# Column tiles of the input projection computed by pairs in seven block products, with weight sums made by accumulating loads

## The chip, the cores and the metric

The kernel runs on one core of a Trainium2 chip. The metric is the device time of one execution in microseconds, the median of several runs. The engines are TensorE (PE, matmul), VectorE (DVE), ScalarE (ACT), GpSimd (Pool) and SyncE (SP); SP and Pool also issue DMAs, Pool through a queue whose descriptors it writes itself, and all DMAs share the core's 16 DMA engines.

## The reference

One layer of a hybrid decoder over 528 prompt tokens (16 of them meta tokens) and 32 sample tokens (8 sequences of 4):

```python
h = rmsnorm(x, g_pre)                                       # 560 x 2048
q, k, v, ga, cb, cc, ch, gc, ma, mc = split(h @ w_in)        # 2048 x 12288
a = stick_breaking(q, k, v) * silu(ga)                       # 8 heads of 128; the samples read 4 cached pages each
c = cb * causal_conv3(cc * ch) * silu(gc)                    # 1024 channels
m = sigmoid(ma + b_ga) * (a @ w_pa) + sigmoid(mc + b_gc) * (c @ w_pc)
x = x + rmsnorm(m @ w_out, g_post)
```

The sections q, k, v, ga, cb, cc, ch, gc are 1024 columns wide, ma and mc 2048. Everything is in float32. The keys, the values and the last rows of the conv's input are outputs too.

## The kernel before

Activations lie transposed in SBUF: `h_hi` and `h_lo` are [128, 16, 560], model width on the partitions in 16 contraction tiles, tokens along the free dimension. Each float32 value is kept as hi + lo, two numbers in TensorE's fp32r format, and a product is three matmuls: whi·h_hi, whi·h_lo, wlo·h_hi.

`proj(c, ranges)` makes one column tile of 128 columns of `h @ w_in`. `weights` (L180) loads the tile's weights as two blocks of 1024 x 128 (512 KB each, issued by SP into one of three `raw` buffers), casts hi on ACT (L188) and subtracts lo on DVE (L189), into one of four hi and lo buffers. `gemm_into` (L192) then runs 16 contraction tiles x 3 matmuls for each of two token ranges, 96 matmuls of 128 x 272 or so (L201), into two PSUM blocks. 256 such 1024 x 128 blocks of weights are split this way.

In the order of the program: the norm; the eight `ga` tiles; eight heads (k, v, q tiles, then the prompt's attention, whose chain of log, sums over keys, exponent and product with the values is L396 to L460); the tile pair cc, ch of conv channel tile 0 (`conv_in(0)`); a loop over 16 pairs of gate tiles `ma`, `mc`, which stores the gates in DRAM (`gate_scr`) and after each column tile takes one step of the generator `decode_steps`; the other conv tiles (`conv_in(1)` to `conv_in(7)`), then `gc` and `cb` for each of 8 channel tiles. Decode reads the pages of the cache: for each of 8 sequences the queries are broadcast to all partitions (`qb`), each of four pages (`page`, 128 keys x 1024) is multiplied with four queries on DVE, and reduced by head on DVE (L560) or ACT (L556); after that come the softmax-like chain and the products with the value pages.

The conv result `c_raw` stays in SBUF and is split to `c_hl` in place; attention's result is loaded from DRAM (`a_scr`, through `arl`) and split to `a_hl` (L305, L306) beside the last `gc`, `cb` tiles. Then come the tiles of `a @ w_pa` and `c @ w_pc`, two and two in turn, 48 matmuls each, merged with the gates to `m1` and `m2`; the product with `w_out`; norm and residual.

A scheduler places each engine's instructions by priority in the order of the program, as far as buffers and waits allow; pools of the program (`heads`, `gates`, `dec`) hold SBUF, and what a later pool allocates in the same place waits until the earlier is free.

Of the kernel before, what the change touches and what calls it, by code (L numbers as in the profile page):

```python
# [25 lines left out]
MID = 288                # tokens [.., MID) and [MID, T) go to two PSUM banks  # L26
ALL = ((0, MID), (MID, T))
QRY = ((NMETA, MID), (MID, T))           # tokens whose outputs are asked for
CNV = ((NMETA - 2, MID), (MID, T))       # these and the conv history before them
TQ = T - NMETA           # 544  # L30
PQ = SEQ                 # prompt tokens among them
# [5 lines left out]
EPS = 1e-6  # L37
LNEXP = "natural_log_exp_and_others"
# [6 lines left out]
def hybrid_step_kernel(  # L45
# [21 lines left out]
    wraw = ctx.enter_context(tc.tile_pool(name="wraw", bufs=3))  # L67
    whl = ctx.enter_context(tc.tile_pool(name="whl", bufs=4))
# [15 lines left out]
    # -------------------------------------------------------------- constants  # L84
# [17 lines left out]
    def load_x(xt, i):  # L102
        lo, hi = XT[i]
        if i == 0:
            nc.sync.dma_start(xt[0:NMETA, :], meta_tokens)
            nc.sync.dma_start(xt[NMETA:hi, :], xp[0:hi - NMETA, :])
        elif hi <= TP:
            nc.sync.dma_start(xt, xp[lo - NMETA:hi - NMETA, :])
        else:
            nc.sync.dma_start(xt[0:TP - lo, :], xp[lo - NMETA:SEQ, :])  # L110
            nc.sync.dma_start(xt[TP - lo:hi - lo, :], xs)
# [21 lines left out]
    # g_pre on every partition, by a product with ones  # L133
# [70 lines left out]
    def gemm(units, rhs, ranges):  # L204
        """rhs(k) -> (hi, lo) of contraction tile k, by token. Returns a PSUM block per token range."""
# [13 lines left out]
    def parts(outs, ranges, base=0):  # L219
        """(PSUM block, slice of a tile whose column 0 is token `base`) of each range."""  # L220
        return [(o, slice(t0 - base, t1 - base)) for o, (t0, t1) in zip(outs, ranges)]

    # the first two gates start on the first tokens while the others are normalized
    START = ((NMETA, 2 * P), (2 * P, T))
# [21 lines left out]
    # small tables: per-channel columns by a transpose of row-wise loads  # L246
# [25 lines left out]
    # -------------------------------------------------- scratch kept in DRAM  # L272
    sg_scr = dram.tile([H, P, PQ], F32, name="sg_scr")
    a_scr = dram.tile([H, P, PQ], F32, name="a_scr")
    gate_scr = dram.tile([KD, P, 2, TQ], F32, name="gate_scr")
    q_scr = dram.tile([TS, DA], F32, name="q_scr")

    # persistent sample-side pieces
# [3 lines left out]
    v_new = const.tile([TS, H, P], F32, name="v_new")  # L282
# [12 lines left out]
    # ---------------------------------------------------------------- heads  # L295
    ictx = ExitStack()
    yp_ = ictx.enter_context(tc.tile_pool(name="cin", bufs=1))
    gctx = ExitStack()
    gp = gctx.enter_context(tc.tile_pool(name="gates", bufs=2))
# [12 lines left out]
    def natural(raw, nat, nat_s):  # L312
        """raw [128, T] -> nat [128, 5, 128] (prompt rows), nat_s [32, 128] (sample rows)."""
# [10 lines left out]
    # key tile -> (group, column in the group, width, first query token, keys)  # L324
# [10 lines left out]
    def head(h):  # L335
        # k
# [4 lines left out]
        for ob, s in parts(o, ALL):  # L341
            act.copy(kr[:, s], ob)
            split_evac(khi[:, s], klo[:, s], kr[:, s], kr[:, s])
# [7 lines left out]
        # v  # L351
        o = proj(GATE_V + h * P, ALL)
        vr = hp.tile([P, T], F32, name="raw", bufs=1)
        for ob, s in parts(o, ALL):
            act.copy(vr[:, s], ob)
        vn = hp.tile([P, 5, P], F32, name="nat", bufs=1)
        natural(vr, vn, v_new[:, h, :])
# [6 lines left out]
        pool.dma_start(v_sample[0, :, :, h, :].rearrange("b t d -> (b t) d"), v_new[:, h, :])  # L364
        # q, scaled
# [3 lines left out]
        for ob, s in parts(o, QRY):  # L369
            split_evac(qhi[:, s], qlo[:, s], ob, ob, SCALE)  # L370
        qs = hp.tile([P, TS], F32, name="qs", bufs=1)
        act.activation(qs, o[1][:, TP - MID:T - MID], AF.Copy, scale=SCALE)
# [5 lines left out]
        # logits of the new keys for the sample queries  # L378
# [7 lines left out]
        # prompt attention: key tiles by later queries, grouped by PSUM bank  # L386
# [24 lines left out]
        for g in GROUPS:  # L411
# [9 lines left out]
            if g == "C":  # L421
                # sums of the later key tiles, key by key
# [44 lines left out]
    for h in range(H):  # L467
        o = ga_o[h] if h < 2 else proj(GATE_GA + h * P, QRY)
        sg = hp.tile([P, TQ], F32, name="sg", bufs=2)
        for ob, s in parts(o, START if h < 2 else QRY, NMETA):  # L470
# [7 lines left out]
    UP, US = PQ + 2, DB * (DT + 2)  # L478
    C0 = NMETA - 2

    def conv_in(i, y):
        cp = yp_
        """u = cc * ch of channel tile i, its last rows out, y = conv(u) + bias."""
        o = proj(COL_CC + i * P, CNV)
        cc = cp.tile([P, T - C0], F32, name="cc", bufs=1)
        for ob, s in parts(o, CNV, C0):
            act.copy(cc[:, s], ob)
        o = proj(COL_CH + i * P, CNV)
        u = cp.tile([P, UP + US], F32, name="u", bufs=1)
        up = u[:, 0:UP]  # L490
        us = u[:, UP:].rearrange("p (b t) -> p b t", t=DT + 2)
        act.copy(us[:, :, 0:2], stc[:, i, :].rearrange("p (b r) -> p b r", r=2))
        dve.tensor_mul(up[:, 0:MID - C0], o[0], cc[:, 0:MID - C0])
        dve.tensor_mul(up[:, MID - C0:UP], o[1][:, 0:TP - MID], cc[:, MID - C0:UP])
        dve.tensor_mul(us[:, :, 2:], o[1][:, TP - MID:T - MID].rearrange("p (b t) -> p b t", t=DT),
                       cc[:, UP:].rearrange("p (b t) -> p b t", t=DT))
        for yv, uv, sl in ((y[:, 0:PQ], up, lambda q: (slice(None), slice(q, q + PQ))),
# [373 lines left out]
```

## Time and profile before

| | |
|---|---|
| median of 3 runs | 1734.3 us (1733.22 to 1734.79) |
| the profiled execution | span 1736.9 us, 2.6 us above that median (no other time is listed for it) |
| PE busy | 1706.4 us, 98% |
| DVE, ACT, Pool busy | 842.8, 744.7, 202.2 us |
| DMA | 249.87 MB, 144 GB/s over the span |

The time by stages, in us of the span, with PE's busy time in each:

| stage | from, to | PE busy |
|---|---|---|
| norm and first tiles | 0 to 66 | 47.8 |
| heads | 66 to 543 | 477 |
| gates with decode's logits | 543 to 944 | 401 |
| conv_in 1 to 7, rest of decode | 944 to 1147 | 203 |
| gc, cb, then w_pa and w_pc | 1147 to 1536 | 389 |
| w_out, norm, residual | 1536 to 1737 | 188.6 |

A busy share is an average over stages. PE has almost no idle time outside the first and the last stage, so the time of a stage in between is read as a number of matmuls. The granted clock of TensorE was 0.996 over the span. Rows that name a line L give that line of the kernel before.

### The profile page before, as it was taken

To read this page: it belongs to the slowest core of one execution; us is meant where nothing else is said; L and a number is where in the kernel's file an instruction comes from. 1 tells how busy PE (TensorE), PEld (TensorE's weight loads), DVE (VectorE), ACT (ScalarE), POOL (GpSimd) and SP (SyncE) were. 2 spreads that over 40 slices of the span, in tenths; PEclk is the share of its full clock that TensorE was granted. 3 is DMA by queue.
4 is the path that set the end of the run, shared out by engine and by line. 5 is a ranking of instruction groups with operands and counts; after the bars stand their busy time and mean duration, and the time that the engine had idled before them with its cause. 6 is when DMAs were issued, how large, how long until landed. Compare 5 with 4: busy or idle time off the path is not lost.

```text
span 1736.9 us, 32151 instructions
## 1 busy us (share of the span) xinstructions
PE 1706.4 (98%) x12764; PEld 1637.0 (94%) x12764; DVE 842.8 (49%) x2092; ACT 744.7 (43%) x2026; POOL 202.2 (12%) x345
## 2 busy tenths in 40 slices
PE   5999999999999999999999999999999999999997
PEld 4999999999999999999999878899999999999986
DVE  7322554554445999996123222242224554444464
ACT  4322555455454999886223111132223222244543
POOL 5000222122111111111001111010000000000010
PEclk9999999999999999999999999999999999999999
DMA  6333333333325777774343444343233444567584
GB/s 191 94 110 116 88 99 93 87 88 98 99 82 192 247 257 253 248 244 148 111 120 102 166 160 149 121 139 91 80 98 85 137 127 133 164 166 184 174 260 153
DMA packets 302057, 249.87 MB, mean 144 GB/s; under 512 B 9181, under 2 KB 272145, under 8 KB 298721
## 3 DMA queue, kind: packets, MB, share of 16 engines
q1 hardware_dynamic: 278992, 161.89, 32.0%
q0 software_dynamic: 22912, 85.91, 14.2%
q8 instruction: 100, 1.64, 0.4%
q14 instruction: 51, 0.42, 0.1%
q10 hardware_dynamic: 2, 0.01, 0.0%
HBM read 225.42 MB, written 22.36 MB: 143 GB/s over the span
## 4 chain that ended last, share of the span: by engine, by line
PE 95%; DVE 2%; DMA 2%; ACT 0%; issue 0%; SPq 0%; POOLq 0%; POOL 0%; ACTq 0%; DVEq 0%
PE mm L201 83%; PE z L631 2%; PE z L830 2%; PE mm L830 2%; PE z L450 1%; DMA raw<-in_w_out 1%; PE o L460 1%; PE z L396 1%; PE o L830 1%; DMA raw<-in_w_in 1%; DVE hn L164 0%; PE tp L830 0%; PE tp L316 0%; DVE h_lo L177 0%; PE z L785 0%; DVE rtmp L120 0%
## 5 line engine op out<-in xcount | busy, mean ns | idle before, releaser
L201 PE MATMUL mm<-h_hi,wlo 128*128 128x272 f32 (+4 forms) x3072 | 894.1, 291 | 0.0
L201 PE MATMUL mm<-h_hi,whi 128*128 128x272 f32 (+4 forms) x3072 | 892.9, 291 | 0.0
L201 PE MATMUL mm<-h_lo,whi 128*128 128x272 f32 (+4 forms) x3072 | 888.1, 289 | 0.3 <-DVE h_lo L177 0.2
L201 PEld LDWEIGHTS mm<-h_hi,whi 128*128 128x128 f32 x3072 | 580.7, 189 | 9.3 <-issue 6.7
L201 PEld LDWEIGHTS mm<-h_hi,wlo 128*128 128x128 f32 x3072 | 580.0, 189 | 4.1 <-issue 3.4
L201 PEld LDWEIGHTS mm<-h_lo,whi 128*128 128x128 f32 x3072 | 579.2, 189 | 4.8 <-issue 3.4
L189 DVE TENSOR_TENSOR wlo<-raw,whi 128x1024 fp32r<-128x1024 f32 x252 | 308.4, 1224 | 493.7 <-ACT whi L188 492.3
L188 ACT CAST whi<-raw 128x1024 fp32r<-128x1024 f32 x256 | 269.0, 1051 | 518.0 <-PE mm L201 499.8
L556 ACT ACTIVATE junk<-pr 128x128 f32<-128x128 f32 x512 | 150.7, 298 | 7.1 <-DVE pr L553 4.3
L560 DVE CUSTOM_DVE_ANT_0 prod<-page,qb 128x128 f32<-128x128 f32 x512 | 116.2, 285 | 1.0 <-DMA qb<-q_scr 1.0
L201 PE MATMUL mm<-m,whi 128*128 128x288 f32 x512 | 105.8, 301 | 0.0
L556 ACT ACTIVATION_READ_ACCUMULATOR junk<-pr 128x1 f32 x512 | 97.2, 190 | 0.0
L201 PE MATMUL mm<-c_hl,whi 128*128 128x272 f32 x512 | 96.8, 287 | 0.0
L201 PE MATMUL mm<-a_hl,whi 128*128 128x272 f32 x512 | 96.7, 288 | 0.0
L201 PEld LDWEIGHTS mm<-m,whi 128*128 128x128 f32 x512 | 84.0, 193 | 0.0
L553 DVE TENSOR_TENSOR pr<-page,qb 128x1024 f32<-128x1024 f32 x64 | 78.0, 1220 | 6.2 <-ACT junk L556 5.7
L201 PEld LDWEIGHTS mm<-c_hl,whi 128*128 128x128 f32 x512 | 80.7, 188 | 0.0
L201 PEld LDWEIGHTS mm<-a_hl,whi 128*128 128x128 f32 x512 | 80.5, 189 | 0.0
L201 PE MATMUL mm<-m,wlo 128*128 128x288 f32 x256 | 76.6, 299 | 0.0
L201 PE MATMUL mm<-c_hl,wlo 128*128 128x272 f32 x256 | 74.2, 290 | 0.0
L201 PE MATMUL mm<-a_hl,wlo 128*128 128x272 f32 x256 | 73.9, 289 | 0.0
L804 DVE TENSOR_TENSOR wlo<-raw,whi 128x1024 fp32r<-128x1024 f32 x32 | 39.1, 1224 | 38.4 <-ACT whi L803 37.9
(289 smaller groups left out, 1641.6 us busy)
## 6 DMA issues: line engine op xcount, KB each, us to landing
raw<-in_w_in SPq DMA_DIRECT2D x192, 512.0 KB, 3.9
raw<-in_w_out SPq DMA_DIRECT2D x64, 512.0 KB, 4.0
qb<-q_scr POOLq DMA_DIRECT2D x16, 1024.0 KB, 7.1
page<-in_cache_k POOLq DMA_DIRECT2D x32, 512.0 KB, 6.0
page<-in_cache_v POOLq DMA_DIRECT2D x32, 512.0 KB, 5.4
gate_scr<-gt POOLq DMA_DIRECT2D x16, 544.0 KB, 4.6
gt<-gate_scr POOLq DMA_DIRECT2D x16, 544.0 KB, 5.1
raw<-in_w_pa SPq DMA_DIRECT2D x16, 512.0 KB, 3.9
```

Source lines behind the costliest of these rows:

```text
L188: act.copy(hi, raw)
L189: lo_eng.tensor_sub(lo, raw, hi.bitcast(F32))
L201: pe.matmul(o, lhsT=w, rhs=r[:, t0:t1], start=(k == 0 and n == 0), stop=(k == nk - 1 and n == 2))
L396: pe.matmul(zt[:m, c0:c0 + n], lhsT=l[:, s0:s0 + m], rhs=r[:, ts:ts + n], start=(c0 == 0 and i == 0), stop=(i == 2), skip_group_check=True)
L450: pe.matmul(o, lhsT=l, rhs=x, start=False, stop=(i == len(ops) - 1), skip_group_check=True)
L460: pe.matmul(ot[:, ts - NMETA:ts - NMETA + n], lhsT=l[:m, st, :], rhs=x[:m, c0:c0 + n], start=False, stop=(g == GROUPS[-1] and i == 2), ski ...
L553: dve.tensor_mul(pr, kt, qb[0][:, t, :])
L556: act.activation(junk, pr[:, h * P:(h + 1) * P], AF.Copy, accum_out=z_all[:, pg, b, h, t:t + 1])
L560: dve.tensor_tensor_reduce(out=prod, in0=kt[:, h * P:(h + 1) * P], in1=qb[t // 2][:, t % 2, h * P:(h + 1) * P], scale=1.0, scalar=0.0, op0 ...
L631: pe.matmul(po[hf][32 * j:32 * (j + 1), :], lhsT=lhs, rhs=rhs, start=(pg == 0), stop=(pg == NPG), tile_position=(0, 32 * j), skip_group_ch ...
L804: dve.tensor_sub(lo, raw, hi.bitcast(F32))
L830: pe.matmul(po[i], lhsT=l, rhs=r, start=(k == 0 and q == 0), stop=(k == KD - 1 and q == 2))
```

## The change

**Pairs.** Two neighbouring column tiles c1, c2 form a 2 x 2 block product: halves k1, k2 of the model width against two halves of the tokens. In Winograd's form of Strassen's method this needs 7 block products of 24 matmuls in place of 8, with sums of blocks on both sides. The tokens are laid out in two equal halves of 280 (8 meta tokens and 264 more in the first; 8, 248 and the samples in the second). 30 pairs are made so: 16 of the conv's sections and 14 of the gates; gate columns 0 and 1 stay plain tiles (`gate_one`). Sums on the token side (`t_hi`, `t_lo`, three of [128, 8, 274]) are made once, among those four plain tiles, and block (0, 1) of h is overwritten with a difference.

**Sums of weights.** They are not computed on an engine. `w_add` issues a DMA from Pool that adds a block of `w_in` in DRAM onto a block in SBUF (four in each pair, 120 in all, 512 KB each). A pair has five plain loads where two tiles had four, and seven splits where they had four.

```diff
+    def w_add(dst, src):
+        pool.dma_start(dst, src.rearrange("(k p) c -> p k c", p=P), accum_op=ALU.add)
+
+    def pair(c, n):
+        c1, c2, k1, k2 = slice(c, c + P), slice(c + P, c + 2 * P), slice(0, 1024), slice(1024, 2048)
+        s = sp2.tile([P, 8, P], F32, name="s", bufs=2)
+        nc.sync.dma_start(s, win[k1, c2].rearrange("(k p) c -> p k c", p=P))
+        w_add(s, win[k2, c2])                                   # sa
+        w11, w21 = w_load(win[k1, c1]), w_load(win[k1, c2])
+        w_add(w21, win[k1, c1])
+        w12, w22 = w_load(win[k2, c1]), w_load(win[k2, c2])
...
+        x, q, y = mm_ps()[:, :n], mm_ps()[:, :n], o_ps()[:, :n]
...
+        product(x, w_split(w11), rb(0, 0), True, False)
+        product(q, w_split(s), rb(0, 1), True, False)
+        act.activation(y, x, AF.Copy, scale=-1.0)
+        w_add(s, win[k1, c1])                                   # sb
+        product(y, w_split(s), rt(0), False, False)
+        s5 = tmp("s5")
+        act.copy(s5, q)
+        product(x, w_split(w12), rb(1, 0), False, True)
+        s2 = tmp("s2")
+        act.copy(s2, y)
+        yield 0, 0, x
+        product(y, w_split(w21), rt(1), False, False)
+        c22 = tmp("c")
+        dve.tensor_sub(c22, y, s5)
+        yield 1, 1, c22
+        w_add(s, win[k2, c1])                                   # sc
+        product(q, w_split(s), rb(1, 1), False, True)
+        c12 = tmp("c")
+        dve.tensor_sub(c12, q, s2)
+        yield 0, 1, c12
+        product(y, w_split(w22), rt(2), False, True)
+        yield 1, 0, y
```

(The remarks sa, sb, sc are added here.) `product` is 8 contraction tiles x 3 matmuls into one PSUM block, `w_split` the cast on ACT and the subtraction on DVE (L681, L682 of the new kernel).

**Buffers.** Three are set anew: `wraw` 5 (was 3), `whl` 3 (was 4), and the memory for Pool's descriptors is 4096 (was the default).

**Order of the program.** The conv sections come first now (four column pairs, each with cc, ch, gc, cb), then the gate pairs. After four of every five pairs one step of decode is taken (`dec_group`). A step is one half of the columns, one sequence and two of the four queries, so each K page is loaded twice per half, by 256 KB (`kpage`, 3 buffers), and the queries in 32 loads (`qb`, 512 KB).

```diff
-                for pg in range(NPG):
-                    kt = page_tile(kc, b, pg)
...
+            for hf in range(2):
+                cs = slice(hf * 512, (hf + 1) * 512)
+                for b in range(DB):
+                    for tp_ in range(2):
+                        qt = d1.tile([P, 2, 512], F32, name="qb", bufs=2)
...
+                        for pg in range(NPG):
+                            kt = d1.tile([P, 512], F32, name="kpage", bufs=3)
+                            page_load(kt, kc, b, pg, cs)
```

**After the pairs.** The conv result goes to DRAM (`c_scr`) and comes back in 8 loads through two buffers into `c_hl`; then all 16 `w_pc` tiles, with the gates loaded, multiplied and written back, and the rest of decode taken beside them; then `a_hl` is filled in 8 loads through the same two buffers; then all 16 `w_pa` tiles.

```diff
+    for k in range(8):
+        cr = g3.tile([P, 2, TQ], F32, tag="gt", name="cr")[:, 0, :]
+        pool.dma_start(cr, c_scr[k])
+        split_evac(c_hl[:, k, :], c_hl[:, 8 + k, :], cr, cr)
+    for j in range(KD):
...
+        oc = gemm(weights([w_pc[0][:, cs]]), lambda k: (c_hl[:, k, :], c_hl[:, 8 + k, :]), QH)
...
+        pool.dma_start(gate_scr[j][:, 1, :], gt)
+        dec_step(2)
+    dec_step(2)
...
+    for k in range(8):
+        ar = g3.tile([P, 2, TQ], F32, tag="gt", name="ar")[:, 0, :]
+        pool.dma_start(ar[:, 0:PQ], a_scr[k])
+        dve.tensor_copy(ar[:, PQ:TQ], a_s[:, k, :])
+        split_evac(a_hl[:, k, :], a_hl[:, 8 + k, :], ar, ar)
```

**How the order moves.** Pool's queue during decode's logits, before: pages and queries, and now and then a store of a gate tile.

```order
L534 DMA page_6804<-in_cache_k 128x1024
L666 DMA gate_scr_599<-gt_5904 128x1088
L534 ISA
L534 DMA page_6995<-in_cache_k 128x1024
L534 ISA
L534 DMA page_7188<-in_cache_k 128x1024
```

The same queue in the first pairs of the new kernel (`s` and `raw` from `in_w_in` are the accumulating loads, L687):

```order
L687 DMA s_6879<-in_w_in 128x8x128
L524 ISA
L524 DMA kpage_6791<-in_cache_k 128x512
L687 DMA raw_6884<-in_w_in 128x8x128
L687 DMA s_6541<-in_w_in 128x8x128
L524 ISA
L524 DMA kpage_6809<-in_cache_k 128x512
L524 ISA
L524 DMA kpage_6827<-in_cache_k 128x512
L537 DMA qb_7113<-q_scr_604 128x2x512
```

And in the last pairs, where the logits are done:

```order
L687 DMA s_13155<-in_w_in 128x8x128
L687 DMA s_13779<-in_w_in 128x8x128
L744 DMA gate_scr_603<-g_13153 128x544
L687 DMA s_13475<-in_w_in 128x8x128
L687 DMA raw_13784<-in_w_in 128x8x128
L744 DMA gate_scr_603<-g_13154 128x544
L687 DMA s_13475<-in_w_in 128x8x128
L687 DMA s_14009<-in_w_in 128x8x128
```

Four accumulating loads for each pair now stand among the pages and the stores on one queue; the first add of s_13779, the pair after next, stands ahead of the second add of s_13475.

PE at the end of the last head, before: the head's own products (L450, L460) stand singly among matmuls of the next column tiles (L201).

```order
L201 MATMUL mm_5778<-h_lo_87,whi_5767 128x272
L450 MATMUL z_5506<-hi416_5539,neg_u_85 128x400
L450 MATMUL z_5521<-lo512_5586,neg_u_85 128x512
L201 MATMUL mm_5778<-h_hi_86,wlo_5768 128x272
L201 MATMUL mm_5778<-h_hi_86,whi_5773 128x272
L201 MATMUL mm_5778<-h_lo_87,whi_5773 128x272
L201 MATMUL mm_5778<-h_hi_86,wlo_5774 128x272
L201 MATMUL mm_5778<-h_hi_86,whi_5773 128x272
L450 MATMUL z_5506<-lo416_5540,neg_u_85 128x400
```

The same place in the new kernel (L203 is the plain product there, L459 stands for L450):

```order
L203 MATMUL mm_5832<-h_lo_87,whi_5828 128x272
L203 MATMUL mm_5832<-h_hi_86,wlo_5829 128x272
L459 MATMUL z_5537<-hi416_5570,neg_u_85 128x400
L459 MATMUL z_5537<-lo416_5571,neg_u_85 128x400
L459 MATMUL z_5552<-hi512_5616,neg_u_85 128x512
L459 MATMUL z_5552<-lo512_5617,neg_u_85 128x512
L459 MATMUL z_5545<-hi416_5588,neg_u_85 128x272
```

Here the head's last products stand together, 33 rows without another matmul between them, behind all the products of the tiles that were open.

More of the change, by code (lines that the diff above doesn't have):

```diff
@@ L620, in decode_steps @@
                 if pg < NPG:
[L621 removed]
+                    vts = []
+                    for j in range(4):
+                        vt = d2.tile([P, DA], F32, name="vpage", bufs=5)
+                        page_load(vt, vc, 4 * g + j, pg, slice(0, DA))
+                        vts.append(vt)
                 for hf in range(2):
@@ L650, in hybrid_step_kernel, with dec_step @@
     dec = decode_steps()
[L652 removed]
+    dec_at = [None]
+    def dec_step(n=1, until=None):
         for _ in range(n):
[L654 to L666 removed]
@@ new lines, in dec_step, with dec_group, w_load @@
+            if dec_at[0] in ("end", until) and dec_at[0] is not None:
+                return
+            dec_at[0] = next(dec, "end")
+    n_group = [0]
+    def dec_group():
+        n_group[0] += 1
+        if n_group[0] % 5:
+            dec_step(1, "logits")
+    gctx = ExitStack()
+    gp = gctx.enter_context(tc.tile_pool(name="gates", bufs=2))
+    sp2 = gctx.enter_context(tc.tile_pool(name="sums", bufs=1))
+    def w_load(src):
+        raw = wraw.tile([P, 8, P], F32, tag="raw", name="raw")
+        nc.sync.dma_start(raw, src.rearrange("(k p) c -> p k c", p=P))
+        return raw
@@ new lines, in hybrid_step_kernel @@
+    for i in range(0, 8, 2):
+        conv_pair(i)
+    for j in range(2, KD, 2):
+        for w, c in ((0, COL_MA), (1, COL_MC)):
+            gs = [gp.tile([P, 2, HU], F32, tag="cv", name="g", bufs=3).rearrange("p a b -> p (a b)")[:, 0:TQ] for _ in range(2)]
+            for m, half, b in pair(c + j * P, HQ):
+                act.activation(gs[m][:, by_query(m, half)], b, AF.Sigmoid, bias=gate_bias(j + m, w))
+            for m in range(2):
+                gate_out(j + m, w, gs[m])
+            dec_group()
@@ new lines, in hybrid_step_kernel @@
+    m2 = ap_.tile([P, KD, TQ], F32R, tag="m2", name="m2")
+    for j in range(KD):
+        cs = slice(j * P, (j + 1) * P)
+        gt = g3.tile([P, 2, TQ], F32, tag="gt", name="gt")
+        pool.dma_start(gt, gate_scr[j])
+        oa = gemm(weights([w_pa[0][:, cs]]), lambda k: (a_hl[:, k, :], a_hl[:, 8 + k, :]), QH)
+        mt = m1 if j < 8 else m2
+        for ob, s in qparts(oa):
+            dve.tensor_mul(gt[:, 0, s], ob, gt[:, 0, s])
+            dve.tensor_add(gt[:, 0, s], gt[:, 0, s], gt[:, 1, s])
+            split_evac(mt[:, j % 8, s], mt[:, 8 + j % 8, s], gt[:, 0, s], gt[:, 0, s])
```

382 lines of the change are left out of this document (209 added, 173 removed).

## The prediction

> **What bounds the kernel now.** I read the page first: the busy times, then the chain that ended last.
>
> ```profile
> span 1736.9 us, 32151 instructions
> PE 1706.4 (98%) x12764; PEld 1637.0 (94%) x12764; DVE 842.8 (49%) x2092; ACT 744.7 (43%) x2026; POOL 202.2 (12%) x345
> PE 95%; DVE 2%; DMA 2%; ACT 0%; issue 0%; SPq 0%; POOLq 0%; POOL 0%; ACTq 0%; DVEq 0%
> ```
>
> TensorE (PE) is busy for 98% of the span and is 95% of the chain. Nothing but fewer or cheaper matmuls, or its last gaps, can make this kernel faster; any new wait of PE is paid in full. The profiled execution's span is 1736.9 us and its own time is not listed apart from it; it stands 2.6 us (0.15%) above the median of 1734.3 us. I sum differences and add them to the median. 0.2%, about 3.5 us, is what a measurement of this kernel can tell from no change.
>
> Then the chain in order of time, from the end of the heads to the end of the gates, and the windows (span of the window, busy time and count of PE, weight load, DVE, ACT, Pool, then granted PE clock, share of the 16 DMA engines, GB/s).
>
> ```profile
> 543.09 400.27 PE mm L201 x3177
> 540.00:740.00 200.00, 200.00 (x1585) 199.58 (x1584) 179.61 (x832) 170.92 (x891) 27.53 (x51) 1.00 0.76 256
> 1560.00:1570.00 10.00, 10.00 (x79) 9.99 (x78) 3.70 (x4) 3.38 (x9) 1.02 (x2) 1.00 1.16 262
> 1570.00:1580.00 10.00, 7.14 (x51) 6.89 (x51) 3.16 (x4) 4.59 (x12) 0.51 (x1) 0.90 0.86 191
> 1580.00:1590.00 10.00, 10.00 (x61) 10.00 (x61) 3.97 (x5) 4.32 (x15) 0.51 (x1) 0.76 0.57 162
> 1590.00:1600.00 10.00, 10.00 (x78) 9.99 (x77) 4.73 (x5) 4.84 (x11) 1.03 (x2) 1.00 0.59 168
> ```
>
> The first row is one unbroken run of PE: 400.27/3177 = 126.0 ns for one matmul. In the second row VectorE (DVE) is 0.9 busy and the DMA engines 0.76, beside logits of the decode, and PE still loses nothing. The last four rows are a stall of another stage: PE idle for 2.9 us, and in the next 10 us only 61 matmuls where 78 run at full clock, so a short gap costs 17 x 0.126 = 2.2 us more.
>
> **The change part by part.** *The pairs.* Two column tiles took 192 matmuls, 24.2 us; in seven products they take 168, 21.2 us. Thirty pairs (16 of conv, 14 of gates) remove 720 matmuls, 90.7 us, if a pair takes only its PE time. Three things may set it instead.
>
> *DMA traffic.* Rows: bytes and share of each queue, and what moves.
>
> ```profile
> q1 hardware_dynamic: 278992, 161.89, 32.0%
> q0 software_dynamic: 22912, 85.91, 14.2%
> raw<-in_w_in SPq DMA_DIRECT2D x192, 512.0 KB, 3.9
> qb<-q_scr POOLq DMA_DIRECT2D x16, 1024.0 KB, 7.1
> page<-in_cache_k POOLq DMA_DIRECT2D x32, 512.0 KB, 6.0
> gate_scr<-gt POOLq DMA_DIRECT2D x16, 544.0 KB, 4.6
> ```
>
> 32.0% of 1736.9 us over 161.89 MB is 3.43 us of all 16 engines per MB, so a weight load of 512 KB costs 1.80 us. Pool's queue: 14.2% over 85.91 MB, 2.87 us per MB. A pair had 4 weight loads; now it has 5 and 4 accumulating ones. The logits now load each K page twice by halves (128 loads of 256 KB, 33.5 MB) and the queries in 32 loads of 512 KB (16.8 MB): 50.3 MB, 144 us. By the order all of them lie in the first 19.5 pairs (78 of the 120 adds): 7.4 us a pair. Storing c or gates: 0.4 us a conv pair, 1.6 us a gate pair. With A for one accumulating load, a pair needs 5 x 1.8 + 7.4 + 0.4 + 4A = 16.8 + 4A in the first 19.5, and 9.0 + 1.6 + 4A = 10.6 + 4A in the last 10.5. No row shows an accumulating load. Its bounds: 1.8 (a plain load) and 3.6 (source and destination both read, all of it twice the work). I take 2.7: one write as before, two reads for one, three runs of bytes for two. The 16 engines give more than 1.00 of the share as it is counted here (1.16 in the window at 1560); between 1.00 and that I take 1.05 as what they can hold. First pairs: 27.6/1.05 = 26.3 us (22.9 to 29.7), so DMA sets them, not PE; 2.1 us over the 24.2 of before, times 19.5: +41 us (-26 to +107). Last pairs: (10.6 + 10.8)/1.05 = 20.4 us, below PE's 21.2.
>
> The Trainium skill, DMA: Bandwidth & Descriptors, "Anatomy of one DMA — SWDGE (gpsimd) path", gives a load from Pool about 2.0 us and its bytes at 436 GB/s, an estimate of 3.2 us for 512 KB; the trace's pages of that size landed in 6.0 us, so the trace disagrees and decides. By the page's figure an add would land in time for the chain below and the last pairs would take 21.2 us.
>
> *The sums' chain.* One buffer s holds three sums of a pair in turn: sa, then sb by adding onto it once sa's split has read it, then sc.
>
> ```profile
> L189 DVE TENSOR_TENSOR wlo<-raw,whi 128x1024 fp32r<-128x1024 f32 x252 | 308.4, 1224 | 493.7 <-ACT whi L188 492.3
> L188 ACT CAST whi<-raw 128x1024 fp32r<-128x1024 f32 x256 | 269.0, 1051 | 518.0 <-PE mm L201 499.8
> sg<-sg_scr SPq DMA_DIRECT2D x8, 256.0 KB, 2.6
> arl<-a_scr POOLq DMA_DIRECT2D x8, 256.0 KB, 3.0
> L348 POOL DMA_DIRECT2D out<-nat x8: 792/794/824, 156.5 to 475.3; - x8
> L350 POOL DMA_DIRECT2D out<-ks x8: 509/513/513, 160.2 to 479.1; - x8
> ```
>
> A split is 1.05 + 1.22 = 2.3 us. With three buffers for hi and lo, sa's split can start when the previous pair's sc product ends; sb's product is due three products of 24 x 0.126 = 3.02 us after that, 9.07 us. Two splits leave 9.07 - 4.54 = 4.5 us for sb's add. It lands, I estimate, in 3.9 (plain) + 0.9 (A above a plain load) + 0.4 (Pool's queue beside SP's, 3.0 against 2.6) = 5.2 us. In Pool's order the first add of the pair after next stands ahead of it; issuing 512 runs took 0.79 us and 32 runs 0.51, so 1024 runs take about 1.1. Together 6.3, 1.8 us late: 23.0 us a pair in the last 10.5 (21.2 if it lands in time, 23.9 at A = 3.6, which adds 0.9). Against 24.2: -13 us (-31.5 to -3). Queued behind a waiting add on Pool are stores, the next adds and pages. In the first pairs this wait runs beside the DMA-bound time and is not added.
>
> *VectorE.* Seven splits of 1.22 and two evacuating subtractions make 9.3 us a pair; the logits and the conv come on top.
>
> ```profile
> L560 DVE CUSTOM_DVE_ANT_0 prod<-page,qb 128x128 f32<-128x128 f32 x512 | 116.2, 285 | 1.0 <-DMA qb<-q_scr 1.0
> L553 DVE TENSOR_TENSOR pr<-page,qb 128x1024 f32<-128x1024 f32 x64 | 78.0, 1220 | 6.2 <-ACT junk L556 5.7
> L503 DVE SCALAR_TENSOR_TENSOR c_raw<-u,wcv,c_raw 128x512 f32<-128x512 f32 x10 | 7.4, 744 | 0.0
> ```
>
> Logits: 116 + 78, the latter in twice as many instructions, I estimate 88: 204/19.5 = 10.5 us a pair. The conv by rows like the last one, about 11 us for four pairs: 2.8. Sum 22.6 us; at the 0.9 that DVE held at 540 to 740, 25.2 us a pair, under the 26.3 of DMA.
>
> *Boundaries*, where PE has nothing to cover the work.
>
> ```profile
> 508.87 12.85 PE mm L201 x101
> 543.09 1.00 PE mm L201 x8
> L305 ACT CAST a_hl<-arl x8: 642/647/649, 1146.8 to 1166.0; 128x544 fp32r<-128x544 f32 x8
> L306 DVE TENSOR_TENSOR a_hl<-arl,a_hl x8: 716/725/726, 1147.5 to 1166.7; 128x544 fp32r<-128x544 f32 x8
> ```
>
> Head 7's softmax tail ran from 508.87 to 543.09, 34.2 us, among matmuls of conv_in(0) and the first gate; the head's own matmuls in it are 5.6 us. Now the gates' evictions wait for the heads' memory, and by the order only 90 matmuls (11.3 us) are left behind the last QK product. Of the 17.3 us left, some 6 were conv_in(0)'s own splits and conv on ACT and DVE, which are gone: 11 us exposed. Sums of the tokens among four plain tiles: 2 us. c_hl is built by 8 loads through 2 slots: four rounds of about 3.0 (load) + 0.5 (issue) + 0.65 + 0.73 = 4.9 us, 19.5 us, of which the last products and the first hide 3.5: 16. a_hl the same way with the first products running along: 12. Three stops, each with the 2.2 us of lower clock: 6. Sum +47 us (20 if the rounds overlap by half and the five raw buffers take away the stall at 1574; 60 if nothing overlaps).
>
> After the 2.9 us gap the granted clock read 0.90, then 0.76. The Trainium skill, TensorE: Matmul & The Clock Gate, Part 1, halves the clock only after an idle window of about 3.4 us; by it gaps of 2 us at each pair would cost no clock. The trace shows the price after 2.9 us, and none for shorter gaps, which I hold at nothing.
>
> Total: +41 - 13 + 47 = +75, 1734.3 + 75 = 1809 us.
>
> **The rivals.** *R1, faster: adds at a plain load's price.* A = 1.8, landing within 4.5 us: -26 - 31.5 + 47 = -10.5, 1724 us, and 1697 with boundaries of 20. It decides from A = 1.94: 0.1 us of A is worth 19.5 x 0.4/1.05 = 7.4 us. For it: K pages of 128 long runs cost less per MB than weights, and PE ran untouched beside a share of 0.76. Against it: an add must read its destination. *R2: adds at twice the price.* A = 3.6: +107 - 3 + 47 = +151, 1885 us; 1898 with boundaries of 60. For it: as many short runs again, all fetched by Pool's queue. *R3: VectorE sets the first pairs.* A near 2.2 with adds in time: (25.2 - 24.2) x 19.5 = +20, - 31.5 + 47: +35, 1769 us. For it: the 179.61 of 200 us. That the work is not removed is excluded: the order has 712 fewer rows on PE.
>
> **How the numbers follow.** Forecast 0.33; R1 0.28, most of it faster by more than 0.2%; R2 0.21; R3 0.13; dearer still (A above 3.6, or the clock falling in every pair, beyond 1900) 0.05. R1 gives 0.25 faster, 0.03 within 0.2%; the rest, 0.72, is slower. The range goes from R1's low end to a little above R2's high end, 1695 to 1905.
>
> **What would show it.** Right: 12 thousand matmuls less 720 and PE at some 89% busy; in the first 300 us of pairs a DMA share near 1.0 and the chain through s<-in_w_in and raw<-in_w_in; pairs of about 26 us, then about 23 with PE waiting for DMA at sb; a gap near 10 us after head 7 and two of 12 to 16 us at c_hl and a_hl. Wrong: an add landing in 4 us and last pairs of 21 us (R1); a share at 1.0 also in the last pairs (R2); DVE at 0.9 with adds landed before they are needed (R3); boundaries without gaps. The forecast falls if PE is over 97% busy across the pairs.

## The result and the profile after

The changed kernel takes 2235.2 us (median of 5 runs, 2225.24 to 2238.97) against 1733.22 us of the kernel before on the same chip: ratio 1.288, 95% interval 1.286 to 1.291. It is slower by 502 us where I forecast 75, and lies far above the range.

The page of the changed kernel: span, busy times, chain by engine, queues, landings.

```profile
span 2223.6 us, 32312 instructions
PE 1804.4 (81%) x12044; PEld 1678.6 (75%) x12044; DVE 1008.1 (45%) x2328; ACT 905.9 (41%) x2231; POOL 502.6 (23%) x650
PE 44%; issue 20%; DMA 20%; POOL 6%; DVE 5%; ACT 4%; POOLq 0%; SPq 0%; DVEq 0%; ACTq 0%
q0 software_dynamic: 160048, 179.26, 38.3%
q1 hardware_dynamic: 310203, 177.63, 28.4%
...
raw<-in_w_in SPq DMA_DIRECT2D x192, 512.0 KB, 5.3
s<-in_w_in POOLq DMA_DIRECT2D x90, 512.0 KB, 6.8
```

The 720 matmuls are gone (12764 to 12044), yet PE is busy for longer, in matmuls at a lower granted clock (0.80 to 0.83 in the pairs, below), and waits for 19% of the span. Nearly half of the chain is no longer PE: 46% is Pool, transfers, and time in which an engine waits for nothing that the profile shows ("issue"). The packets of Pool's queue rose from 22,912 to 160,048.

Windows of the changed kernel (columns as in the prediction): the end of the heads, early pairs, late pairs.

```profile
520.00:573.00 53.00, 42.96 (x270) 38.54 (x270) 32.72 (x32) 20.43 (x28) 8.22 (x16) 0.81 0.33 88
700.00:900.00 200.00, 131.35 (x840) 125.30 (x840) 104.32 (x368) 92.66 (x325) 58.57 (x67) 0.80 0.85 186
1400.00:1600.00 200.00, 151.65 (x959) 146.04 (x959) 52.05 (x53) 55.28 (x80) 43.12 (x36) 0.83 0.80 152
```

840 matmuls in 200 us are 5 pairs: 40 us each. Late, with DVE 0.26 busy and no logits left, 959 in 200 us are 35 us each. The forecast had 26.3 and 23.0.

The tile c of the changed kernel, one row a pair, gives the mean: (1712.5 - 607.9)/29 = 38.1 us a pair, 13.9 above the 24.2 of before. Thirty pairs make 417 of the 487 us by which the profiled execution is longer (2223.6 against 1736.9). Most of the rest is in the three stops around them, about 59 us: some 157 matmuls are missing at the end of the heads, 173 at c_hl and 146 at a_hl (520 to 573, 1712 to 1760, 1900 to 2020), at 0.124 us each.

```profile
L738 DVE TENSOR_TENSOR c<-mm,s x30: 429/441/447, 607.9 to 1712.5; 128x272 f32<-128x272 f32 x22, 128x274 f32<-128x274 f32 x8
```

The chain of waits in a late pair (start, duration, what):

```profile
1586.27 1.54 POOL s L687
1587.81 5.40 issue
1593.21 0.52 POOL raw L687
1593.72 0.36 issue
1594.09 1.27 POOL gate_scr L744
1595.36 4.61 issue
...
1599.98 7.81 DMA s<-in_w_in
...
1607.87 1.05 ACT whi L681
...
1608.95 1.24 DVE wlo L682
```

This is what the forecast did not have. Adds that stand ready one behind the other start 6.9 us apart (1586.3, 1593.2, 1600.0): Pool is busy for 1.5 us and then stands for 4.6 to 5.4 us in which it waits for nothing that the profile shows. Over the whole run such waits before an add come to 334 us:

```profile
POOL s L687 <- issue: 205.9, 46, 8.6
POOL raw L687 <- issue: 127.9, 25, 6.0
```

### The profile page after: what moved, and what is told of

Its sections match the earlier page's. It is cut to its first block, busy times and chain, and to the rows that moved or that the text cites. A ratio compares the mean times of both kernels' runs of the same rounds, so it can differ in the third digit from the quotient of the medians.

```text
span 2223.6 us, 32312 instructions
## 1 busy us (share of the span) xinstructions
PE 1804.4 (81%) x12044; PEld 1678.6 (75%) x12044; DVE 1008.1 (45%) x2328; ACT 905.9 (41%) x2231; POOL 502.6 (23%) x650
## 3 DMA queue, kind: packets, MB, share of 16 engines
q0 software_dynamic: 160048, 179.26, 38.3%
## 4 chain that ended last, share of the span: by engine, by line
PE 44%; issue 20%; DMA 20%; POOL 6%; DVE 5%; ACT 4%; POOLq 0%; SPq 0%; DVEq 0%; ACTq 0%
PE mm L203 32%; DMA s<-in_w_in 15%; PE z L631 3%; POOL s L687 2%; ACT whi L681 2%; POOL kpage L524 2%; DVE wlo L682 2%; DMA kpage<-in_cache_k 2%; DMA raw<-in_w_in 2%; PE z L1000 2%; PE mm L713 1%; PE mm L1000 1%; DMA out<-ln 1%; ACT junk L550 1%; PE z L459 1%
## 5 line engine op out<-in xcount | busy, mean ns | idle before, releaser
L713 PE MATMUL o<-t_hi,whi 128*128 128x272 f32 (+1 forms) x720 | 244.2, 339 | 219.6 <-ACT whi L681 209.4
L713 PE MATMUL mm<-h_hi,whi 128*128 128x272 f32 (+1 forms) x960 | 310.1, 323 | 111.2 <-ACT whi L681 108.1
L203 PE MATMUL mm<-h_hi,whi 128*128 128x272 f32 (+3 forms) x1152 | 335.9, 292 | 7.9 <-ACT g L754 5.3
L203 PE MATMUL mm<-h_lo,whi 128*128 128x272 f32 (+3 forms) x1152 | 335.3, 291 | 1.2 <-DVE h_lo L179 1.2
L203 PE MATMUL mm<-h_hi,wlo 128*128 128x272 f32 (+3 forms) x1152 | 334.8, 292 | 0.0
L713 PE MATMUL mm<-h_hi,wlo 128*128 128x272 f32 (+1 forms) x960 | 300.6, 313 | 17.4 <-DVE wlo L682 17.4
L713 PE MATMUL mm<-h_lo,whi 128*128 128x272 f32 (+1 forms) x960 | 300.6, 313 | 0.0
L682 DVE TENSOR_TENSOR wlo<-s,whi 128x1024 fp32r<-128x1024 f32 x90 | 110.2, 1225 | 404.8 <-ACT whi L681 404.7
L681 ACT CAST whi<-s 128x1024 fp32r<-128x1024 f32 x90 | 94.1, 1045 | 439.2 <-DMA s<-in_w_in 390.7
L191 DVE TENSOR_TENSOR wlo<-raw,whi 128x1024 fp32r<-128x1024 f32 x132 | 161.6, 1225 | 203.1 <-ACT whi L190 187.7
L687 POOL DMA_DIRECT2D s<-in_w_in x90 | 143.2, 1591 | 486.6 <-issue 205.9
L713 PE MATMUL o<-t_lo,whi 128*128 128x272 f32 (+1 forms) x720 | 236.6, 329 | 0.0
L713 PE MATMUL o<-t_hi,wlo 128*128 128x272 f32 (+1 forms) x720 | 235.1, 327 | 1.6 <-DVE wlo L682 1.6
L203 PEld LDWEIGHTS mm<-h_hi,whi 128*128 128x128 f32 x1152 | 218.4, 190 | 9.8 <-ACT g L754 6.0
L203 PEld LDWEIGHTS mm<-h_lo,whi 128*128 128x128 f32 x1152 | 217.8, 189 | 2.2 <-DVE h_lo L179 1.4
L203 PEld LDWEIGHTS mm<-h_hi,wlo 128*128 128x128 f32 x1152 | 217.6, 189 | 0.2
```

Source lines behind the costliest of these rows:

```text
L191: lo_eng.tensor_sub(lo, raw, hi.bitcast(F32))
L203: pe.matmul(o, lhsT=w, rhs=r[:, t0:t1], start=(k == 0 and n == 0), stop=(k == nk - 1 and n == 2))
L681: act.copy(hi, x)
L682: dve.tensor_sub(lo, x, hi.bitcast(F32))
L687: pool.dma_start(dst, src.rearrange("(k p) c -> p k c", p=P), accum_op=ALU.add)
L713: pe.matmul(o, lhsT=l[:, k, :], rhs=r, start=(start and k == 0 and m == 0), stop=(stop and k == 7 and m == 2), skip_group_check=True)
```

## The experiments

An add's price A is worked out in all of them in one way: q0's share times the span, less 349.6 us for Pool's other traffic (20.0% of f3's 1748.2 us, which has no adds), over 120. In the changed kernel: (851.6 - 349.6)/120 = 4.18 us of all 16 engines, and (160,048 - 35,248)/120 = 1040 packets an add, one for each run of 512 B and 16 more. The subtraction supposes that Pool's other traffic costs the same in every run. SP's queue cost 3.50 us per MB in f3 and 3.54 to 3.61 in the runs with 120 more loads from Pool, so I estimate that it is good to about 0.1 us of A.

**What an add costs: room for descriptors, and adding.** e1 is the control of e2.

```diff
-    wraw = ctx.enter_context(tc.tile_pool(name="wraw", bufs=5))
+    wraw = ctx.enter_context(tc.tile_pool(name="wraw", bufs=3))      # e1, e2; kpage 3 -> 2, pr 2 -> 1
-SCRATCH = 4096
+SCRATCH = 16384                                                      # e2
```

> The changed kernel with fewer buffers (raw 3 for 5, K pages 2 for 3, the decode's products 1 for 2), the control for e2. Theory: in the pairs Pool's in-order queue with adds about 6.9 us apart sets the time, not the prefetch of weights; so within 2% of the changed kernel, 2200 to 2280 us. Rival (weights arrive too late): over 2300.

> e1 with 16384 in place of 4096 for the memory of Pool's descriptors. Theory ring: Pool waits until the descriptors of an earlier add are fetched; with four times the room adds start under 3 us apart where they stood back to back, a pair loses 3 x 4 us or more of its 35 to 39, and the time falls to 1850 to 2000 us. Rival writing: Pool needs some 6.9 us to write the 1024 descriptors of an add; spacing and time stay within 2% of e1.

e1 took 2225.9 us, as the changed kernel; e2 2091.8, 134 us less. (In both the order spreads the decode's logits over all pairs.) Windows of e1 and of e2 over the same 900 us:

```profile
600.00:1500.00 900.00, 587.95 (x3954) 566.18 (x3953) 392.43 (x1189) 360.54 (x1122) 242.93 (x253) 0.81 0.83 173
```

```profile
600.00:1500.00 900.00, 666.50 (x4542) 642.34 (x4540) 448.65 (x1367) 420.05 (x1299) 282.75 (x297) 0.85 0.96 201
```

With room, the share of the DMA engines is 0.96 instead of 0.83. The waits for nothing visible before the adds to s, first e1, then e2:

```profile
POOL s L687 <- issue: 230.9, 45, 9.4
```

```profile
POOL s L687 <- issue: 11.1, 1, 11.1
```

From 560 us on no two adds of the changed kernel start nearer than 6.6 us to each other, and none of e1 nearer than 6.7; in e2 the nearest are 1.5 us apart. Pool's timeline in e2 shows three adds 3.2 and 2.7 us apart:

```profile
1462.08 1.57 POOL L687 DMA_DIRECT2D raw<-in_w_in  x1 [7.43 <-ACT whi L681]
...
1465.24 1.56 POOL L687 DMA_DIRECT2D s<-in_w_in  x1 [1.01 <-ACT whi L681]
...
1467.99 2.29 POOL L687 DMA_DIRECT2D s<-in_w_in  x1
```

Only the size of the memory differs. So the 6.9 us were a wait for room, not Pool's time to write descriptors: the ring theory holds. But it is worth 134 us, not the 226 to 376 that I expected. In e2 the work of the DMA engines nearly fills a pair: A there is (834.5 - 349.6)/120 = 4.04 us, a pair (decode over all 30) needs 9.0 + 4.8 + 1.0 + 16.2 = 31.0 us of them and took 33.3.

> The changed kernel with each accumulating load reading 128 runs of 4 KB in place of 1024 runs of 512 B, the same bytes (it adds other weights, so the sums are not those of the products). Theory ring and rival writing: an eighth of the descriptors, adds under 3 us apart, 1800 to 1950 us. Rival bytes: what costs is the adding of 512 KB in the DMA engines, landing stays 6 to 7 us and the time above 2150.

> e3 between: each accumulating load reads 512 runs of 1 KB, the same bytes (other weights are added, so the sums are not those of the products). With 1024 packets an add took 4.2 us of the 16 engines and the time was 2235, with 128 of 4 KB 2.85 us and 1990. Theory packets: price and time fall with their number: half of them takes 3.4 to 3.6 us, 2070 to 2120 us. Rival (anything below 4 KB is as dear): 2200 and more.

> The changed kernel with the accumulating loads replaced by plain loads of the same blocks from Pool (the sums of weights are left out: each takes its last block alone). Theory ring: the descriptors are as many, so adds stay 5 to 7 us apart and the time within 5% of 2235. Rival bytes: reading the destination is the cost; landing falls from 6.7 to about 4 us and the time to 1850 to 2000 us.

```diff
-        pool.dma_start(dst, src.rearrange("(k p) c -> p k c", p=P), accum_op=ALU.add)
+        pool.dma_start(dst.rearrange("p k c -> p (k c)"), win[0:P, 0:1024], accum_op=ALU.add)        # e3
+        pool.dma_start(dst.rearrange("p (k a) c -> p k (a c)", a=2),
+                       win[0:512, 0:256].rearrange("(k p) c -> p k c", p=P), accum_op=ALU.add)       # h3
+        pool.dma_start(dst, src.rearrange("(k p) c -> p k c", p=P))                                  # e4
```

Pool's queue on the pages of e3, h3, e4 and f3 (no adds, below), in this order:

```profile
q0 software_dynamic: 52528, 179.26, 34.8%
```

```profile
q0 software_dynamic: 98608, 179.26, 36.4%
```

```profile
q0 software_dynamic: 52528, 179.26, 29.6%
```

```profile
q0 software_dynamic: 35248, 116.33, 20.0%
```

| each of the 120 loads | packets | Pool busy, us | A, us | time, us | us a pair |
|---|---|---|---|---|---|
| adds, 1024 runs of 512 B (changed kernel) | 1040 | 1.58 | 4.18 | 2235 | 38.1 |
| adds, 512 runs of 1 KB (h3) | 528 | 1.33 | 3.23 | 2033 | 31.4 |
| adds, 128 runs of 4 KB (e3) | 144 | 0.89 | 2.85 | 1990 | 29.9 |
| plain, 1024 runs of 512 B (e4) | 144 | 0.90 | 1.78 | 1903 | 27.1 |

Each load moves 512 KB, but none of h3, e3 and e4 computes the layer: e4 leaves the sums out, and h3 and e3 read one and the same block of weights each time. So the length of the runs and the place that they are read from change together there, and these runs do not part the two.

e3 (1990) fell between its theory (1800 to 1950) and its rival (above 2150). h3 came out 37 us below its bracket. e4 came within its rival's range, but its loads landed in 6.1 us, not 4. The theory of packets holds in its direction, though not in proportion: halving the packets saves 0.95 us, the other 384 only 0.38. The rival of bytes is half right: adding itself, in long packets, costs 1.07 us more than a plain load.

By these rows the other 1.33 us are paid only where a load adds. A base load of s from SP, which adds nothing, also goes out in 1040 packets (q1 has 31,200 packets more for 30 of them than in f3), and a load of that size from SP cost 1.80 us before, on the mean of its queue, or 2.17 if all that q1 takes here beyond f3 is put down to these 30; Pool's plain load in 144 packets costs 1.78. For plain loads the packets made little difference, for accumulating ones 1.33 us.

The times in the table hold the room as well as the price. The 334 us of waits for nothing visible before an add are 9.8 us in h3, 19.5 in e3 and 20.7 in e4, all with 4096. So of the 202 us between the changed kernel and h3 some 134 may be room, by e1 and e2, and the rest price; that is an estimate. My expectation for e4, 5 to 7 us between loads because the descriptors are as many, failed; the trace counts packets, not descriptors.

**What the sums cost, whoever makes them.** The four raw blocks of a pair lie in SBUF, so an engine can add them.

```diff
-        nc.sync.dma_start(s, win[k1, c2].rearrange("(k p) c -> p k c", p=P))
-        w_add(s, win[k2, c2])
-        w11, w21 = w_load(win[k1, c1]), w_load(win[k1, c2])
-        w_add(w21, win[k1, c1])
-        w12, w22 = w_load(win[k2, c1]), w_load(win[k2, c2])
+        w11, w21, w22, w12 = (w_load(win[a, b]) for a, b in ((k1, c1), (k1, c2), (k2, c2), (k2, c1)))
+        pool.tensor_add(s, w21, w22)            # f1; dve.tensor_add in f2; none in f3
+        pool.tensor_add(w21, w21, w11)          # and so the two later sums
```

> The changed kernel with the four sums of weights of a pair computed by Pool from the four raw blocks, which lie in SBUF anyway: four plain loads a pair, no accumulating load, no base load. A subtraction of this size on Pool took 2.3 to 3.3 us, so four are 10 to 13 us of a pair. Theory (the adds' transfer and their queue were the price): pairs of 23 to 26 us, 1800 to 1880 us. Rival (the split and evacuation chain of the seven products is the price, whoever sums): pairs over 27 us, above 1900.

> As f1 with the sums on VectorE: 4 x 1.22 = 4.9 us more a pair, 14.2 us beside 10.5 us of decode and 2.8 of conv in the first pairs, 27.5 at full use. Theory: first pairs 28 to 30 us, last 21 to 23; 1830 to 1900 us. Rival (chain of the seven products): above 1900 with DVE under 0.8 busy.

> The changed kernel with the sums of weights left out: four plain loads a pair, and sa, sb, sc and the sum of w21 replaced by splits of raw blocks; seven splits and seven products remain. It is what the pairs cost without any price for sums. Theory: 21.5 to 24 us a pair, 1730 to 1790 us, the rest above before being the boundaries (about 50 to 90 us). Rival: if the seven splits with decode set the time, 25 us and more in the first pairs, above 1800.

f1: 1897.2 us, 26.9 a pair. f2: 1765.3, 22.6 a pair. f3: 1750.9 (ratio 1.008, 1.005 to 1.012), 22.1 a pair. f3 leaves the sums out and does not compute the layer. f2 computes all of it, takes 1.017 of the time before (1.013 to 1.021) and is 470 us faster than the changed kernel: making the sums by accumulating loads was nearly all of the loss. DVE sums cost only 14 us above none, and f2 came out 65 us below its bracket, though f2's DVE is 0.94 busy from 600 to 1200:

```profile
600.00:1200.00 600.00, 571.63 (x4437) 563.41 (x4436) 564.07 (x1533) 427.19 (x1348) 112.54 (x198) 0.99 0.61 185
```

f1 fell between theory and rival, at another price: DVE's own instructions grew longer beside Pool's sums. Groups of f1:

```profile
L682 DVE TENSOR_TENSOR wlo<-raw,whi 128x1024 fp32r<-128x1024 f32 x120 | 210.5, 1758 | 29.0 <-ACT whi L681 29.0
L553 DVE CUSTOM_DVE_ANT_0 prod<-kpage,qb 128x128 f32<-128x128 f32 x512 | 202.6, 443 | 0.7 <-DMA kpage<-in_cache_k 0.7
```

1758 and 443 ns, where in f2, which differs only in the engine that makes the sums, they are 1216 and 283.

> The changed kernel with plain tiles in place of the pairs (eight block products, no sums of weights or of tokens); the order of sections, the decode's steps, the conv result by way of DRAM, the buffers and the separate loops of w_pc and w_pa stay. It prices these by themselves. Theory: 48 us of boundaries as forecast and up to 40 more: 1780 to 1820 us. Rival: if they cost nothing, 1735; if decode beside the tiles is slower in the new form, above 1850.

f4 took 1848.8 us, but answers less than I wanted: without the tokens' sums their memory was free, and the order moved the decode's logits forward, from 330 us on, among the heads (534 matmuls from 500 to 600 us, where 800 fit). It is not the change without pairs, and no price is taken from it.

**The round through the sum buffers.** The chain above returns once a pair through s: sc's split, base load, the next first add. I took that round for the cause of the 35.6 us.

```diff
-        s = sp2.tile([P, 8, P], F32, name="s", bufs=2)
+        s = sp2.tile([P, 8, P], F32, name="s", bufs=3)      # g1: e1 with it; g2: and SCRATCH 12288; h1: wraw 4
```

> e1 with three buffers for the sums s in place of two. In the last pairs of the changed kernel the chain of waits goes round once a pair: sc's split frees s, the base load of the pair after next, its first add, then in Pool's order the other three adds 6.9 us apart, sc's landing and split: 35.6 us. Theory loop: with a third buffer the first add no longer waits for the split of the same round; what is left is four adds and stores at 6.9 us, about 28 us, and the time falls by 50 to 150 us from 2226 to 2080 to 2180. Rival (DMA engines full at 0.8 to 0.9 of the share as counted, whoever waits for whom): within 1% of 2226.

> g1 with 12288 for the memory of Pool's descriptors, beside e2 with 2092 (two buffers, 16384). Theory: loop and spacing both gone, DMA engines left: A of 4.1 us gives 16.8 + 16.4 = 33.2 us of all engines in the first pairs and 27 in the last, at a share of 0.95 35 and 28.5 us, 30 us less than e2 or somewhat more: 2000 to 2070. Rival: loop the greater part, below 1980.

> The changed kernel with three buffers for the sums and four raw buffers for five; the decode keeps its place in the first two thirds of the pairs. Theory round (in the last pairs the first add waits for the split of the same round): the last pairs fall from 35.6 to about 28 us, four adds at 6.9 us, and the time by some 80 us to 2130 to 2170. Rival (only the descriptors' room and the adds' transfer count): last pairs stay above 34 us, time within 1.5% of 2235.

> The changed kernel with the decode's logits left out (set to zero): no K pages, no queries, none of their work on VectorE and ScalarE. Theory adds: a pair is then 35 to 36 us everywhere, as in the last pairs, so only (39.4 - 35.6) x 19.5 = 74 us go, 2140 to 2180 us. Rival (DMA engines are full in the first pairs, 7.4 us a pair of logits count in full at the share of 0.83): 19.5 x 8.9 = 174 us go, 2040 to 2080.

g1: 2226.6 us, as e1. g2: 2105.2, no better than e2 (2091.8, with more memory for descriptors) and above both of its brackets. h1 keeps the decode in the first two thirds as the changed kernel does: 2152.3, inside the theory's range, but not for its reason. Its 83 us are mostly not where the theory had them. Windows of h1 in early and late pairs, then of h2 in the same two:

```profile
700.00:1200.00 500.00, 349.20 (x2249) 334.69 (x2250) 289.84 (x1069) 259.32 (x925) 166.29 (x192) 0.82 0.93 205
1300.00:1600.00 300.00, 214.54 (x1511) 207.28 (x1511) 80.99 (x81) 88.17 (x126) 65.39 (x53) 0.85 0.83 155
```

```profile
700.00:1200.00 500.00, 351.25 (x2278) 337.19 (x2279) 154.50 (x212) 124.19 (x188) 95.70 (x74) 0.82 0.73 133
1300.00:1600.00 300.00, 222.04 (x1440) 213.50 (x1440) 77.57 (x78) 84.48 (x121) 63.26 (x51) 0.84 0.80 151
```

Late, 1511 matmuls in 300 us are 33.4 us a pair, not 28; the changed kernel had 1411 there, 35.7. The greater gain came early, 37.4 us a pair where the changed kernel took 41.1 (2249 matmuls against 2046 from 700 to 1200), at a DMA share of 0.93 where it was 0.85. So the theory of the round fell as the main cause; it has at most 2.3 us of a late pair. Pool's timeline in h1's late pairs:

```profile
1503.11 1.57 POOL L687 DMA_DIRECT2D s<-in_w_in  x1 [7.30 <-DVE wlo L682]
1512.35 1.56 POOL L687 DMA_DIRECT2D raw<-in_w_in  x1 [7.68 <-issue]
1521.78 1.57 POOL L687 DMA_DIRECT2D s<-in_w_in  x1 [7.87 <-DMA s<-in_w_in]
1522.67 1.27 POOL L744 DMA_DIRECT2D gate_scr<-g  x1
1528.76 1.55 POOL L687 DMA_DIRECT2D s<-in_w_in  x1 [4.81 <-issue]
1538.03 1.56 POOL L687 DMA_DIRECT2D s<-in_w_in  x1 [7.12 <-DVE wlo L682]
```

The adds of a pair go one after the other, each 7 to 9 us behind the last, whether the gap is put down to room, to a split or to a landing: four of them are a pair. h2, without the logits, says the same: 2159.2 us, as the theory of the adds had it (2140 to 2180), with 2278 matmuls in 500 early us and 1440 in 300 late ones, 36.9 and 35.0 us a pair. Its early pairs are that slow at a DMA share of 0.73, so it is not full DMA engines that set them. Which of the small waits between adds is the longer in a late pair, room or s, these runs do not part.

**The gaps, and a better kernel.** Windows of f3, 322 matmuls fit in each: the heads' end, c_hl, a_hl.

```profile
520.00:560.00 40.00, 31.31 (x174) 26.89 (x173) 23.17 (x26) 15.53 (x22) 6.36 (x13) 0.74 0.22 69
1240.00:1280.00 40.00, 29.90 (x172) 27.37 (x173) 21.31 (x39) 23.60 (x29) 15.00 (x24) 0.74 0.65 218
1420.00:1460.00 40.00, 29.54 (x168) 26.59 (x168) 17.31 (x36) 11.02 (x17) 6.78 (x13) 0.79 0.55 164
```

452 matmuls are missing, 57 us. A fourth place shows no gap. The 128 products of decode with the value pages (L631), which stand beside w_pc now, keep PE busy for 18 us longer. Their row in the kernel before, then in f3:

```profile
L631 PE MATMUL z<-page,A_all 128*32 128x512 f32 x128 | 37.3, 597 | 0.0
```

```profile
L631 PE MATMUL z<-vpage,A_all 128*32 128x512 f32 x128 | 55.2, 598 | 0.0
```

One of them is as long as before (598 ns), so they overlap less; why was not tested.

> f2 (sums on VectorE) with two of the three gaps filled: c_hl from eight buffers loaded at once, and a_hl's prompt part built beside the tiles of w_pc, so that only the samples' columns are left at the end. In f2 each of the two stretches of 40 us ran some 170 matmuls where 322 fit, 18 to 19 us lost. Theory: 25 to 35 us come back, 1730 to 1740 us. Rival (the work only moves, DVE and ACT are the bound there): above 1755.

> g3 with the gates' buffers taken before the heads, so that the first plain tiles can be evicted and run among head 7's last products, as before. Head 7's stretch in f2 lost about 18 us. Theory: 12 to 18 us less than g3, 1715 to 1728 us, under the kernel before. Rival (the tail then only delays the sums of the tokens): within 5 us of g3.

```diff
+    crp = crx.enter_context(tc.tile_pool(name="crp", bufs=8))     # g3: c_hl from eight buffers
+        if 2 <= j < 10:                                           # g3: in the loop of w_pc
+            k = j - 2
+            ar = g3.tile([P, 2, TQ], F32, tag="gt", name="ar")[:, 0, 0:PQ]
+            pool.dma_start(ar, a_scr[k])
+            split_evac(a_hl[:, k, 0:PQ], a_hl[:, 8 + k, 0:PQ], ar, ar)
+    cvp = ictx.enter_context(tc.tile_pool(name="cvp", bufs=3))    # g4: the gates' buffers, ahead of the heads
```

g3 took 1720.7 us, 44.5 less than f2 and more than I expected: 0.8% below the kernel before (ratio 0.992, 0.9904 to 0.9937), a small gain but clear of the noise. It computes the whole layer. The two windows that were filled had lost 38 us in f3; in g3 the L631 products also took 36.5 us of PE again, which I had not forecast. g4 took 1726.3 us (0.9948, 0.9932 to 0.9963), 5.6 more than g3, as neither the theory nor its rival had it. Windows of g4, the last of them then in g3:

```profile
520.00:560.00 40.00, 38.72 (x297) 37.72 (x296) 27.77 (x33) 25.82 (x33) 5.50 (x14) 1.00 0.31 93
560.00:580.00 20.00, 11.45 (x80) 10.81 (x79) 20.00 (x13) 9.87 (x11) 0.54 (x1) 0.87 0.32 93
1240.00:1260.00 20.00, 12.65 (x94) 12.16 (x94) 10.92 (x18) 13.55 (x20) 6.98 (x14) 0.86 0.66 218
```

```profile
1240.00:1260.00 20.00, 17.24 (x137) 17.02 (x136) 9.64 (x10) 8.89 (x14) 3.01 (x6) 1.00 0.55 156
```

The heads' end is filled, and PE waits some 20 us later for DVE, which is busy without a break with the sums of the tokens and of the first pairs' weights. That is only part of a move: at the end of the pairs g4 is still 6 us ahead of g3 (the last c starts at 1248.4 against 1254.3). It loses 11 us behind that, where c_hl's gap is wide again, 94 matmuls against 137 in those 20 us. Why the gates' buffers do this was not tested.

## Why the prediction was wrong

Two steps failed: the price of an add, and the pace at which Pool can start adds, which I had at 1.1 us, with the room for descriptors at nothing. The second weighs more. With A = 4.18 put into my sum for the DMA engines, the pairs take 31.9 and 26.0 us, and with the boundaries as forecast the total is 1734.3 + 151 + 19 + 47, about 1951 us, an estimate; some 285 us are still missing. At the shares that were measured, (16.8 + 16.7)/0.85 = 39.4 and (10.6 + 16.7)/0.80 = 34.1 us, near the 40 and 35 found. So the engines' work for a pair was sized nearly right but for A; that they would be kept full was the error.

- *What bounds the kernel; 720 matmuls, 90.7 us.* Right: they are gone, and where the sums are made by VectorE or left out a pair takes 22.6 or 22.1 us, near the 21.2 of PE alone.
- *An add at A = 2.7 us (1.8 to 3.6).* 4.18 us, above both bounds. I priced adding by the byte; here it also costs by the packet, 2.85 us in 144 packets and 4.18 in 1040. That 2.85 is near my 2.7 is luck: my kernel never sent such packets. The number of packets was not the surprise, since plain loads from SP have as many.
- *1.1 us for the add ahead on Pool's queue.* Wrong in kind. Pool was busy 1.58 us, but the next add starts 6.9 us later, since there is no room for its descriptors. I listed the memory for descriptors among the buffers of the change and put no price on it; it is worth 134 us (e1 against e2).
- *The chain of sb, 6.3 against 4.5 us.* Too short: landing 6.8 us, behind an add 6.9 us earlier. I had built the landing from SP's 3.9 us, although my own rows had loads of this size from Pool at 6.0. Late pairs 35 us, not 23.0; which wait between two adds decides there stays open.
- *A DMA share of 1.05.* 0.85 with the small room, 0.93 with a third sum buffer, 0.96 with room (windows of 200 to 900 us): none of these reached 1.05.
- *VectorE sets the pairs (R3).* Not in the changed kernel, at 0.52 busy in the early window. It does nearly so in f2.
- *Gaps of 2 us in each pair at no loss of clock.* The gaps became longer, and the granted clock fell to 0.80 over the pairs. The rule of the Trainium skill, TensorE: Matmul & The Clock Gate, Part 1, a halved clock after an idle window of about 3.4 us, goes with it: from 600 to 1712 us PE stood 36 times for 4.5 to 14.7 us. While PE waits for sums anyway, this clock should decide little; no run shows what it costs.
- *Boundaries +47.* Near in size: about 59 us in the changed kernel and 57 in f3, 18 to 19 in each of the three places. c_hl cost what I had forecast with its 2 us for the clock, a_hl some 5 us more. Of the tail after head 7 I had 11 plus 2 for the clock; about 18 was lost. The slower products with the value pages, 18 us, had no term.
- *The rivals.* R2 came nearest, with dear adds, but its sign, a DMA share of 1.0 also in the last pairs, did not show (0.80). No rival had the room for descriptors. The 0.05 for "dearer still" was far too small: with no row for an operation, two bounds from other operations are not a range.

The Trainium skill, DMA: Bandwidth & Descriptors, "Anatomy of one DMA — SWDGE (gpsimd) path", gave an estimate of 3.2 us for 512 KB from Pool; plain loads landed in 6.1 us (e4), the adds in 6.8 us.

## What to carry to other kernels

An operation that no trace shows is priced by a run of its own before work is built on it; here one kernel with 120 of them would have told. Count the runs of an accumulating load and not only its bytes, and read the time between the starts of two DMAs on Pool's queue, not Pool's busy time. The block products paid here once the sums were made by VectorE (14 us in all) and two of the gaps at the stage borders were filled, and then by 0.8% of the 5% that 720 matmuls are: what the borders lose can be as large as the gain.

## What the hardware showed that I had not expected

- An accumulating load from Pool sent 1040 packets where a plain one from Pool of the same runs sent 144, and took 4.18 against 1.78 us of all DMA engines. A plain load from SP sent 1040 packets too, and cost 1.80 us on the mean of its queue in the kernel before.
- With 4096 for the descriptors' memory, no two adds of 1024 runs started nearer than 6.6 us to each other; with 16384 they did down to 1.5 us.
- Additions of two SBUF tiles on Pool (2.5 to 3.1 us each) made three of DVE's groups with two SBUF inputs 1.4 to 1.6 times as long on the mean, against f2 (wlo<-raw, prod, pr), and a fourth 1.09 times (wlo<-s).
